# Joint 512-column matmuls for the fourth block product of the first MLP product, with its bank filled by ScalarE

## The chip, the cores and the metric

The kernel runs on one core of a Trainium2 chip. The metric is the device time of one execution in microseconds (us). One execution was also taken by the profiler; its span runs from its first instruction to its last.

## The reference, cut to what matters

One decoder layer over 512 positions with 1024 features, in float32: a combined input projection feeding a gated recurrence (HGRN2) and a block-sparse attention (MoBA), an output projection, cross-attention into 256 memory tokens, and an MLP. The change lies in the first matrix product of the MLP:

```python
h = rms_norm(x, norm_mlp[l])
x = x + jnp.square(jax.nn.relu(h @ w_ff1[l])) @ w_ff2[l]   # w_ff1: 1024 x 4096, w_ff2: 4096 x 1024
return rms_norm(x, norm_final)
```

## The kernel before

All large products work on split operands. A float32 matrix is written as an upper part, rounded to the fast matmul type (float32r), and a lower part, the rest. A product is then upper x upper, plus upper weights x lower activations, plus lower weights x upper activations. ScalarE makes the upper part of a weight tile (`wh<-w...` in the profile), VectorE subtracts it for the lower part (`wl<-w...,wh`).

The first MLP product, `h @ w_ff1`, is done with a Strassen-Winograd scheme: seven block products instead of eight. The 1024 input features, the 512 positions and the output columns are each cut in two. The work goes in eight groups, `f1_group(j)`, j = 0 to 7. A group makes all seven products p = 0 to 6 for two tiles of 128 weight columns (index b); each product sums over 512 input features, four tiles of 128 (index k). In groups 0 to 6 the products come in the order 0, 1, 2, 5, 4, 3, 6 (`F1_ORDER`); group 7 takes them in their own order. The "third" and "fourth" product are p = 2 and p = 3. Some weight blocks are sums, made by VectorE (`f1_add`) or by accumulating DMA transfers issued by GpSimd.

An activation operand `op1(p, k)` holds its upper part in 256 columns and its lower part in the 256 columns behind it. The accumulators are four tiles of two PSUM banks each, `Z`, `Y`, `XA` and `XB` (X is XA in even groups, XB in odd ones), seen as [128, 2, 512] with `lo` the first and `hi` the last 256 columns of each bank. The upper weight part is used in one of two ways (`upper`):

- joint: one matmul of 512 columns for each tile. Upper x upper lands in `lo`, upper x lower in `hi`, and both halves are added when the bank is read;
- not joint (p = 1 and 3, both in Y): two matmuls of 256 columns with the same weights, both into `lo`.

The lower weight part (`lower`) is a 256-column matmul into `lo` in either case. So a joint product has 16 matmuls and another 24. `lower_first` and `lower_last` decide whether `lower` or `upper` goes first.

Products share banks because the scheme adds them. X holds product 0, then 0+2, then 0+2+4, then 0+2+4+6. After product 0, ScalarE copies X to Z, where product 5 is added. Y holds product 1 and then 1+3. What a group leaves goes to two result tiles, `t1` and `t2` (in the profile `g`): after each product `evac(p)` has ScalarE copy one half of a bank and VectorE add other halves. `f1_tile` multiplies a finished tile by the norm's factor `rb3` with max or min (the relu, with either sign), and a square on ScalarE follows.

The order on each engine is the order in which the code issues it. Every product is a step: `need(w)` issues the split of the weights for the step after the next one, and loads of coming raw tiles; then come these lists, in this order: `post` (squares on ScalarE, by `f1_post`), a VectorE sum of weights at the third step, `first` (VectorE additions that free a bank soon), the held lower parts of the split, and `rest` (other VectorE work, by `f1_rest`). Then the step's matmuls are issued and `evac(p)`. The raw weight tiles `wA`, `wB`, `wc`, `wC`, `wD` have three buffers in each of two pools. A load into one waits until the split's lower part (or the sum) that reads its former content is done; loads go through SyncE's queue in order, accumulating transfers through GpSimd's (lines 373 and 375). GpSimd (line 240) and SyncE (line 237) also issue sums of w_ff2's blocks in DRAM, for the next stage. Most other instructions of the trace have line 118, that of a recording helper, so the groups are told apart by tile names.

Of the kernel before, what the change touches and what calls it, by code (L numbers as in the profile page):

```python
# [11 lines left out]
AF = mybir.ActivationFunctionType  # L12
ALU = mybir.AluOpType
AX = mybir.AxisListType

P = 128
# [109 lines left out]
def hybrid_layer(ctx: ExitStack, tc: tile.TileContext, xT, memT, ws, vecs, consts, rots, out):  # L126
    nc = tc.nc
    pace = Pace()
    V, A, PE = (pace.engine(e, t) for e, t in ((nc.vector, "dve"), (nc.scalar, "act"), (nc.tensor, "pe")))
# [7 lines left out]
    first = ExitStack()  # L137
# [101 lines left out]
    def add(dst, src):  # L239
        return nc.gpsimd.dma_start(dst, src, accum_op=ALU.add, max_dma_last_dim=4 * D)  # L240
# [73 lines left out]
    def load_unit():  # L314
        u = state["load"]
        raws[u] = raw_tile(f"wr{u}", u >= FF2 and (u - FF2) % 2 == 1)
        if len(sources[u].shape) == 3:
            SY.dma_start(raws[u].rearrange("p (n c) -> p n c", n=4), sources[u])
        else:
            SY.dma_start(raws[u], sources[u])  # L320
        state["load"] += 1
        for _ in range(sums_after(u)):
            more_sums()
# [34 lines left out]
    def split_unit(eng=None):  # L358
        u = split_begin()
        split_part(u, 0, D, eng)  # L360
        del raws[u]
# [7 lines left out]
    def f1_load(j, what):  # L369

        r, c = {"A": (0, 0), "B": (0, 0), "C": (1, 1), "D": (1, 0)}[what.upper()]
        t = f1raw[what, j] = raw_tile(f"w{what}{j}", what in "AD")
        nc.sync.dma_start(two(t), E[r][c][j].rearrange("n p c -> p n c"))
        if what in "Bc":
            nc.gpsimd.dma_start(two(t), E[0][1][j].rearrange("n p c -> p n c"), accum_op=ALU.add)
# [4 lines left out]
    def f1_prep(j, s):  # L380

        split_raw(split_begin(), f1raw[("ABACcDd" if j == 7 else "ABADcCD")[s], j], 0, D)
        if s == 1 and j == 0:
            f1_add(j, "A", "B", "C")
        if j == 7:
            if s == 1:
                f1_load(j, "d")
                state["load"] = FF2
            elif s > 3:
                load_unit()  # L390
        elif s == 1:
            f1_load(j + 1, "B")
        elif s == 2:
            f1_load(j + 1, "A")
        elif s == 4:
            f1_load(j + 1, "c")
        elif s == 5:
            f1_load(j + 1, "C")
        elif s == 6:
            f1_load(j + 1, "D")  # L400
        if s == 2 or s == 6 and j > 1:
            more_sums()

    def need(u):
        marks.append(last_mm[0])
        if MLP <= u + SPLIT_AHEAD < FF2:
            f1_prep(*divmod(u + SPLIT_AHEAD - MLP, 7))
            return
        last = MLP if u < MLP else UNITS
        most = RAWS if u < MLP else 2 * RAWS  # L410
        want_load, want_split = min(last, u + LOAD_AHEAD + 1), min(last, u + SPLIT_AHEAD + 1)
        while state["split"] < want_split or state["load"] < want_load:
            if state["load"] < want_load and state["load"] - state["split"] < most:
                load_unit()
            elif state["split"] < want_split:
                split_unit()
            else:
                break
        if MLP - 6 <= u < MLP - 2:
            for what in ("A", "B", "cC", "D")[u - MLP + 6]:  # L420
                f1_load(0, what)
        if MLP - 7 <= u < MLP - 2:
            more_sums()
# [124 lines left out]
    eps = cpool.tile([P, 1], F32, name="eps")  # L548
# [48 lines left out]
    for i in range(2):  # L597
        t = fp.tile([P, NT, P], F32, name=f"AT{i}")
# [694 lines left out]
    half = T // 2  # L1293
# [59 lines left out]
    def part(k, h):  # L1353

        return g[k][:, :, h * half:(h + 1) * half]

    rest = []

    def f1_tile(t, op):
        V.scalar_tensor_tensor(t, t, 0.0, rb3[:, None, :].to_broadcast([P, 2, T]), op0=op, op1=ALU.mult)  # L1360
        post.append(lambda: A.activation(t, t, AF.Square))

    def f1_end(t, j):
        k = j // 2
        f1_tile(t, ALU.max)
        if j % 2:
            subs.append(lambda: V.tensor_sub(part(k, 1), part(k + 4, 1), part(k, 1)))

    post, first, subs = [], [], []

    def f1_post():
        while post:
            post.pop(0)()

    def f1_rest():
        while rest:
            rest.pop(0)()

    lower_last = [False]

    def f1_group(j):

        X = XX[j % 2]
        t1, t2 = (g[4 * i + j // 2][:, 2 * j % 4:2 * j % 4 + 2, :] for i in range(2))
        lo, hi = slice(0, half), slice(half, T)

        def evac(p):
            def add(when, to, acc, *parts):
                for x in parts:
                    when.append(lambda x=x: V.tensor_add(to, to, acc[:, :, x]))  # L1390

            if p == 0:
                A.activation(Z, X, AF.Copy)
            elif p == 1:
                A.activation(t2[:, :, hi], Y[:, :, lo], AF.Copy)
            elif p == 2:
                A.activation(t2[:, :, lo], X[:, :, lo], AF.Copy)
                add(first, t2[:, :, lo], X, hi)
            elif p == 5:
                A.activation(t1[:, :, lo], Z[:, :, lo], AF.Copy)  # L1400
                add(rest, t1[:, :, lo], Z, hi)
            elif p == 4:
                add(first, t2[:, :, hi], X, lo, hi)
            elif p == 3:
                add(rest, t2[:, :, lo], Y, lo)
            else:
                A.activation(t1[:, :, hi], X[:, :, lo], AF.Copy)
                add(rest, t1[:, :, hi], X, hi)
                rest.append(lambda: f1_end(t1, j))
            if p == (4 if j == 7 else 3):  # L1410
                rest.append(lambda: f1_tile(t2, ALU.min))

        every = range(4)
        steps = [(p, every) for p in F1_ORDER[j]]
        if j == 0:
            steps[1:3] = [(1, range(3)), (2, range(3)), (1, range(3, 4)), (2, range(3, 4))]
        for p, ks in steps:
            at_p = F1_ORDER[j].index(p)
            if at_p == 3 and j == 0:
                nc.scalar.preload_act_table_set("natural_log_exp_and_others")  # L1420
            w = MLP + 7 * j + at_p
            if j == 0 and at_p == 4:
                drain("n3")
            if 0 in ks:
                held.append([])
                need(w)
                f1_post()
                if at_p == 2:
                    D = "Dd"[j == 7]
                    f1_add(j, D, D, "A")  # L1430
                while first:
                    first.pop(0)()
                for made_low in held.pop():
                    made_low()
                f1_rest()
                if at_p == 3 and subs:
                    subs.pop()()
                if j == 7 and at_p in (3, 5):
                    need_op(at_p // 5)
                if at_p == 5 and j < 7:  # L1440
                    f1_add(j + 1, "A", "B", "C")
                if j == 0 and at_p == 2:
                    step(made["n3"])
                    set_wait(made["n3"], 1e6)
            acc = {1: Y, 3: Y, 5: Z}.get(p, X)
            joint = p not in (1, 3)
            opens = 0 in ks and p < 2
            tiles = [(b, op1(p, k), slice(b * T + k * P, b * T + k * P + P)) for b in range(2) for k in ks]

            def upper():  # L1450
                for b, a, c in tiles:
                    first_of = opens and c.start % T == 0
                    if joint:
                        mm(acc[:, b], his[w][:, c], a, first_of, False)
                    else:
                        for x in lo, hi:
                            mm(acc[:, b, lo], his[w][:, c], a[:, x], first_of and x is lo, False)

            def lower():
                for b, a, c in tiles:  # L1460
                    mm(acc[:, b, lo], los[w][:, c], a[:, lo], False, False)

            lower_first = lower_last[0] and not opens
            for half_of in (lower, upper) if lower_first else (upper, lower):
                half_of()
            lower_last[0] = not lower_first
            if 3 in ks:
                evac(p)

# [175 lines left out]
    for p, (name, begins, after) in enumerate(PLAN):  # L1647
# [3 lines left out]
        for j in range(8):  # L1651
# [10 lines left out]
            hi, lo = his[FF2 + i], los[FF2 + i]  # L1662
# [3 lines left out]
            for part_of in parts:  # L1666
# [13 lines left out]
                opens = begins and c == 0 and part_of is parts[0]  # L1680
# [91 lines left out]
```

## Time and profile before

| | |
|---|---|
| median of 3 runs | 720.58 us |
| the three runs | 720.26, 720.58, 725.79 us |
| profiled execution, its own time | 719.96 us |
| its span | 718.1 us |
| TensorE busy in the span | 709.5 us (99%) |
| VectorE busy | 581.1 us (81%) |
| ScalarE busy | 451.4 us (63%) |
| GpSimd busy | 81.5 us (11%) |
| the first MLP product, all eight groups | 395.15 to 553.38 us, 158.23 us |

In the profile PE is TensorE's matmuls, PEld its weight loads, DVE VectorE, ACT ScalarE, POOL GpSimd, SPq SyncE's queue. A row of a group of instructions gives the operation, the tile written `<-` the tiles read (buffer numbers left out), the shape, the count, and times in us or, where they are those of one instruction, in ns. A row of the timeline gives start and length in us, and in brackets the engine's idle time before it and what ended that. TensorE's matmuls are pipelined, and a row's length covers their overlap.

### The profile page before, as it was taken

The page shows a single profiled execution, that of the slowest core. Times are in us where ns is not written, and L with a number is a line of the kernel's source. Part 1 is how long each engine was busy: PE and PEld are TensorE (multiplying, and loading weights), DVE is VectorE, ACT ScalarE, POOL GpSimd, SP SyncE. Part 2 cuts the span into 40 slices and gives each one's busy share as a digit, 9 for nine tenths or more (in the row PEclk, how much of TensorE's full clock was granted, in tenths as well). Part 3 has the DMA queues.
Part 4 walks back from the last instruction along what each step waited for, and adds up shares of the span by engine and source line. Part 5 has one row for each costly group of instructions (what it writes and reads, how often), then busy time and mean ns, then how long its engine had stood idle before and what let it go on. Part 6 is the DMA issues. An engine that isn't in the chain of part 4 may idle for free.

```text
span 718.1 us, 10752 instructions
## 1 busy us (share of the span) xinstructions
PE 709.5 (99%) x4038; PEld 613.2 (85%) x4038; DVE 581.1 (81%) x882; ACT 451.4 (63%) x654; POOL 81.5 (11%) x98
## 2 busy tenths in 40 slices
PE   9999999999999999999999999999999999999995
PEld 7888888888888888888888999999999888888885
DVE  6899537898787777767578889989899799987886
ACT  7883585446586577656565866565657665547672
POOL 2511132000000000000011111211111100110000
PEclk9999999999999999999999999999999999999998
DMA  9999699976457846453757588898899976998623
GB/s 298 273 298 303 160 177 251 364 263 141 157 174 203 259 158 193 153 177 117 235 135 162 148 204 188 221 288 244 261 237 272 301 268 199 278 279 248 191 74 117
DMA packets 63843, 155.58 MB, mean 217 GB/s; under 512 B 5264, under 2 KB 21008, under 8 KB 63280
## 3 DMA queue, kind: packets, MB, share of 16 engines
q1 hardware_dynamic: 47920, 116.43, 46.8%
q0 software_dynamic: 14592, 37.75, 28.8%
q10 hardware_dynamic: 1280, 0.72, 0.3%
q8 instruction: 31, 0.51, 0.3%
q14 instruction: 20, 0.16, 0.1%
HBM read 152.79 MB, written 48.23 MB: 280 GB/s over the span
## 4 chain that ended last, share of the span: by engine, by line
PE 98%; DMA 1%; DVE 0%; ACT 0%; DVEq 0%; SPq 0%; issue 0%; ACTq 0%
PE Y L118 16%; PE X L118 12%; PE xo L118 8%; PE XB L118 6%; PE XA L118 6%; PE mkq L118 6%; PE xq L118 6%; PE wo L118 6%; PE mv L118 3%; PE hg L118 3%; PE hq L118 3%; PE Z L118 3%; PE hf L118 3%; PE memX L118 3%; PE hi L118 3%; PE memY L118 2%
## 5 line engine op out<-in xcount | busy, mean ns | idle before, releaser
L118 DVE TENSOR_TENSOR wl<-wr,wh 128x1024 fp32r<-128x1024 f32 (+2 forms) x139 | 165.6, 1197 | 31.0 <-ACT wh L118 28.2
L118 ACT ACTIVATE wh<-wr 128x1024 fp32r<-128x1024 f32 (+2 forms) x139 | 142.8, 1036 | 74.9 <-PE Y L118 14.5
L240 POOL DMA_DIRECT2D u<-in_ws_dram x32 | 28.6, 903 | 358.3 <-PE memX L118 108.6
L118 PE MATMUL X<-op,wh 128*128 128x512 f32 (+1 forms) x264 | 62.9, 385 | 0.0
L118 PEld LDWEIGHTS X<-op,wh 128*128 128x128 f32 x264 | 47.2, 189 | 8.5
L118 PE MATMUL Y<-op,wh 128*128 128x512 f32 x192 | 47.2, 391 | 0.0
L118 PEld LDWEIGHTS Y<-op,wh 128*128 128x128 f32 x192 | 35.0, 188 | 6.6
L118 PEld LDWEIGHTS X<-op,wl 128*128 128x128 f32 x256 | 33.5, 191 | 1.6
L118 PE MATMUL X<-op,wl 128*128 128x256 f32 x256 | 34.1, 282 | 0.0
L118 PE MATMUL Y<-OS,wh 128*128 128x256 f32 x256 | 33.4, 283 | 0.0
L118 PEld LDWEIGHTS Y<-OS,wh 128*128 128x128 f32 x256 | 32.5, 192 | 0.7
L118 DVE TENSOR_TENSOR op<-g,op 128x1024 fp32r<-128x1024 f32 x24 | 29.3, 1219 | 2.8 <-ACT op L118 2.8
L118 ACT ACTIVATE op<-g 128x1024 fp32r<-128x1024 f32 x28 | 29.3, 1045 | 0.6 <-PE XB L118 0.6
L118 ACT ACT_TABLE_LOAD x20 | 25.7, 1283 | 2.2 <-issue 1.8
L118 PEld LDWEIGHTS Y<-op,wl 128*128 128x128 f32 x192 | 25.3, 191 | 1.3
L118 PE MATMUL Y<-op,wl 128*128 128x256 f32 x192 | 25.7, 282 | 0.0
L118 PE MATMUL xq<-x1hi,wl 128*128 128x512 f32 x64 | 25.6, 400 | 0.0
L118 PE MATMUL mkq<-xhi,wh 128*128 128x512 f32 x64 | 25.4, 397 | 0.0
L118 PE MATMUL mkq<-xhi,wl 128*128 128x512 f32 x64 | 25.4, 397 | 0.0
L118 PE MATMUL xq<-x1hi,wh 128*128 128x512 f32 x64 | 25.3, 396 | 0.0
L118 DVE TENSOR_TENSOR wl<-wD,wh 128x1024 fp32r<-128x1024 f32 x15 | 18.4, 1225 | 8.5 <-ACT wh L118 7.9
L118 PE MATMUL mkq<-xlo,wh 128*128 128x512 f32 x64 | 25.2, 394 | 0.0
(370 smaller groups left out, 1914.3 us busy)
## 6 DMA issues: line engine op xcount, KB each, us to landing
wr<-in_ws_dram SPq DMA_DIRECT2D x87, 512.0 KB, 4.9
u<-in_ws_dram POOLq DMA_DIRECT2D x32, 512.0 KB, 8.1
wr<-u SPq DMA_DIRECT2D x32, 512.0 KB, 4.6
u<-in_ws_dram SPq DMA_DIRECT2D x16, 512.0 KB, 10.9
wr<-m SPq DMA_DIRECT2D x16, 512.0 KB, 4.1
m<-in_ws_dram POOLq DMA_DIRECT2D x12, 512.0 KB, 10.1
m<-in_ws_dram POOLq DMA_DIRECT2D x16, 256.0 KB, 6.5
wA<-in_ws_dram SPq DMA_DIRECT2D x8, 512.0 KB, 6.4
```

What stands on the lines that cost most here:

```text
L118: return f(*args, **kw)
L240: return nc.gpsimd.dma_start(dst, src, accum_op=ALU.add, max_dma_last_dim=4 * D)
```

## The change

It has five parts. Joint matmuls for product 3 in groups 0 to 6, and for product 1 in group 0. In groups 1 to 6 ScalarE fills `lo` of Y with zeros at the group's first step, product 1 accumulates onto them instead of opening the bank, and after product 2 ScalarE copies `hi` of X into `hi` of Y, where product 3 is then added: with that, `hi` of X need not be added by VectorE any more, and that addition goes. This copy and the one of `lo` of X to t2 are put on `post`, so they stand behind the next step's split. In group 0, where Y is opened by a joint product 1, its `hi` is added to t2 by VectorE. After product 3 both halves of Y are added, on `first` instead of `rest`. And the square of t1 goes to a list of its own, run after the following group's second `evac`.

```diff
-    def f1_tile(t, op):
+    def f1_tile(t, op, when):
...
-        post.append(lambda: A.activation(t, t, AF.Square))
+        when.append(lambda: A.activation(t, t, AF.Square))
...
-        f1_tile(t, ALU.max)
+        f1_tile(t, ALU.max, ready if j < 7 else post)
...
             elif p == 1:
                 A.activation(t2[:, :, hi], Y[:, :, lo], AF.Copy)
+                if j == 0:
+                    add(rest, t2[:, :, hi], Y, hi)
             elif p == 2:
-                A.activation(t2[:, :, lo], X[:, :, lo], AF.Copy)
-                add(first, t2[:, :, lo], X, hi)
+                if 0 < j < 7:
+                    post.append(lambda: A.activation(Y[:, :, hi], X[:, :, hi], AF.Copy))
+                    post.append(lambda: A.activation(t2[:, :, lo], X[:, :, lo], AF.Copy))
+                else:
+                    A.activation(t2[:, :, lo], X[:, :, lo], AF.Copy)
+                    add(first, t2[:, :, lo], X, hi)
...
             elif p == 3:
-                add(rest, t2[:, :, lo], Y, lo)
+                add(first if j < 7 else rest, t2[:, :, lo], Y, *((lo, hi) if j < 7 else (lo,)))
...
-                rest.append(lambda: f1_tile(t2, ALU.min))
+                rest.append(lambda: f1_tile(t2, ALU.min, post))
...
                 need(w)
+                if p == 0 and 0 < j < 7:
+                    A.activation(Y[:, :, lo], eps[:, :, None].to_broadcast([P, 2, half]), AF.Copy, scale=0.0)
                 f1_post()
...
-            joint = p not in (1, 3)
-            opens = 0 in ks and p < 2
+            joint = j == 0 or p != 1 and (j < 7 or p != 3)
+            opens = 0 in ks and (p == 0 or j in (0, 7) and p == 1)
...
-            lower_first = lower_last[0] and not opens
+            lower_first = lower_last[0] and p > 1
...
             if 3 in ks:
                 evac(p)
+                while behind:
+                    behind.pop(0)()
+                behind.extend(ready)
+                ready.clear()
```

More of the change, by code (lines that the diff above doesn't have):

```diff
@@ L1357, in hybrid_layer @@
     rest = []
-    def f1_tile(t, op):
+    def f1_tile(t, op, when):
         V.scalar_tensor_tensor(t, t, 0.0, rb3[:, None, :].to_broadcast([P, 2, T]), op0=op, op1=ALU.mult)
-        post.append(lambda: A.activation(t, t, AF.Square))
+        when.append(lambda: A.activation(t, t, AF.Square))
     def f1_end(t, j):
         k = j // 2
-        f1_tile(t, ALU.max)
+        f1_tile(t, ALU.max, ready if j < 7 else post)
         if j % 2:
             subs.append(lambda: V.tensor_sub(part(k, 1), part(k + 4, 1), part(k, 1)))
-    post, first, subs = [], [], []
+    post, ready, behind, first, subs = [], [], [], [], []
     def f1_post():
```

## The prediction

> **What bounds the kernel now.** I began with the page: what is busy, and which engine carries the chain that ended last.
>
> ```profile
> span 718.1 us, 10752 instructions
> PE 709.5 (99%) x4038; PEld 613.2 (85%) x4038; DVE 581.1 (81%) x882; ACT 451.4 (63%) x654; POOL 81.5 (11%) x98
> PE 98%; DMA 1%; DVE 0%; ACT 0%; DVEq 0%; SPq 0%; issue 0%; ACTq 0%
> ```
>
> TensorE is busy for 99% of the span and holds 98% of the chain. The other engines matter only where they make it wait. Then I cut the changed stage, the first MLP product, into its eight groups (j = 0 to 7) by windows. Columns: window, its length, busy time of each engine with instruction counts, granted clock, DMA share, GB/s. The rows are j = 2, 3 and 4 and the sum of all eight.
>
> ```profile
> 435.26:454.95 19.69, 19.69 (x129) 18.06 (x129) 18.05 (x19) 12.10 (x14) 4.24 (x4) 1.00 0.83 211
> 454.95:474.63 19.68, 19.68 (x129) 18.05 (x129) 16.34 (x17) 12.10 (x14) 3.37 (x3) 1.00 0.95 251
> 474.63:494.32 19.69, 19.69 (x130) 18.06 (x129) 18.68 (x20) 12.10 (x14) 2.39 (x2) 1.00 0.95 257
> sum 158.23, PE 158.21 PEld 144.86 DVE 141.87 ACT 101.97 POOL 24.70; mean PE 19.78 PEld 18.11 DVE 17.73 ACT 12.75 POOL 3.09
> ```
>
> The stage takes 158.23 us and TensorE is busy for 158.21 of it, at clock 1.00. So there is no wait here to be won. Only TensorE's own work can shrink, and only a new wait can cost. VectorE is nearly full (up to 18.68 of 19.69), ScalarE is not (12.1), and the DMA share reaches 0.95.
>
> **TensorE, step by step.** The chain lists each product of a group as one row: start, length, bank, matmuls. These are j = 3 from product 0 on, and above them the end of j = 2.
>
> ```profile
> 449.27 2.87 PE Y L118 x24
> 452.15 2.80 PE XA L118 x16
> 454.95 2.77 PE XB L118 x16
> 457.71 2.88 PE Y L118 x24
> 460.59 2.80 PE XB L118 x16
> 463.39 2.77 PE Z L118 x16
> 466.16 2.80 PE XB L118 x16
> 468.96 2.87 PE Y L118 x24
> ```
>
> Products 1 and 3 (bank Y) are the 24-matmul steps: 16 of 256 columns for the weights' upper part, 8 of 256 for the lower part. The others run 8 of 512 and 8 of 256. A 256-column matmul thus takes 2.875/24 = 0.1198 us. A step of 2.77 leaves (2.77 - 8 x 0.1198)/8 = 0.2265 us for a 512-column one. Two of the first cost 0.2396 us, one of the second 0.2265: 0.0131 us saved per pair. Steps that begin with the lower part take 2.80 instead of 2.77. Product 3 begins with the upper part, after a product that ended with the upper part, exactly as product 5 (Z) does, so 2.77 is its row. The order of parts stays as it was in every group: I walked the new condition (p > 1) through j = 0, 1 and 7, and it gives the old sequence.
>
> **What the change removes on TensorE.** Product 3 becomes joint in j = 0 to 6, product 1 in j = 0: 8 products, 64 pairs. By steps: 8 x (2.87 - 2.77) = 0.80 us. By pairs: 64 x 0.0131 = 0.84 us. A second reading, busy time of the groups by shape:
>
> ```profile
> L118 PE MATMUL Y<-OS,wh 128*128 128x256 f32 x256 | 33.4, 283 | 0.0
> L118 PE MATMUL Z<-OB,wh 128*128 128x512 f32 x64 | 15.8, 389 | 0.0
> ```
>
> 2 x 33.4/256 - 15.8/64 = 0.0141 us, or 0.90 us for 64 pairs. I take **0.8 us**, with 0.7 and 0.9 as ends. That all 158 us are TensorE-bound makes this gain arrive in full if nothing new waits.
>
> The Trainium skill (TensorE: Matmul & The Clock Gate, Back-to-back issue gap) gives an isolated warm matmul of N columns N/2.4 + 2.5 ns. By this rule a pair would save only the fixed 2.5 ns, and the whole change about 0.16 us, an estimate from that page. The trace does not agree: by it both kinds of step would take about 2.6 us, 0.02 apart, where the chain has 2.87 and 2.77.
>
> **What it adds on ScalarE.** In j = 1 to 6: a fill of Y's first half (2 x 256 columns) with zeros, and a copy of X's second half into Y. The trace has no fill, so I bound it: below by the smallest write into Y, above by a write of twice the size; nearest is the 512-element copy.
>
> ```profile
> L118 ACT ACTIVATE Y<-x,vec x3: 462/462/463, 703.1 to 708.7; 128x256 f32<-128x256 f32 x3
> L118 ACT ACTIVATE g<-XA x8: 598/598/604, 403.6 to 533.7; 128x512 f32<-128x512 f32 x8
> L118 ACT ACTIVATE Z<-XA x4: 1006/1008/1008, 398.0 to 516.9; 128x1024 f32<-128x1024 f32 x4
> ```
>
> I take 0.60 us for each, ends 0.46 and 1.01. That is 1.2 us a group on an engine with 7.6 us idle, so only the places count. Here is ScalarE through j = 3, with TensorE's first matmuls of products 1, 2 and 4.
>
> ```profile
> 454.99 0.60 ACT L118 ACTIVATE g<-XA 128x512 f32<-128x512 f32 x1 [4.61 <-PE XA L118]
> 455.48 1.05 ACT L118 ACTIVATE wh<-wA 128x1024 fp32r<-128x1024 f32 x1
> 456.71 1.06 ACT L118 ACTIVATE g<-g 128x1024 f32<-128x1024 f32 x1 [0.18 <-DVE g L118]
> 457.55 2.08 PE L118 MATMUL Y<-OS,wh 128*128 128x256 f32 x16
> 457.81 1.01 ACT L118 ACTIVATE Z<-XB 128x1024 f32<-128x1024 f32 x1
> 460.43 1.12 PE L118 MATMUL XB<-OS,wl 128*128 128x256 f32 x8
> 460.67 0.58 ACT L118 ACTIVATE g<-Y 128x512 f32<-128x512 f32 x1
> 466.00 1.12 PE L118 MATMUL XB<-OS,wl 128*128 128x256 f32 x8
> ```
>
> - **The fill** stands behind the split of wA (ends 456.53) and ahead of the square of t2. It runs 456.53 to 457.13. Product 1 starts at 457.55: **0.42 us to spare**, and with the long end, 1.01, still 0.01. This is a new wait of TensorE, and it is the thinnest place. Queued behind the fill on ScalarE are the square of t2 and the copy Z<-XB.
> - **VectorE** gives the fill its go: the two additions out of Y now come first in the last step of a group, ahead of the split's lower part instead of one addition behind it.
>
> ```profile
> 409.33 1.22 DVE L118 TENSOR_TENSOR wl<-wD,wh 128x1024 fp32r<-128x1024 f32 x1 [1.45 <-ACT wh L118]
> 453.60 1.22 DVE L118 TENSOR_TENSOR wl<-wB,wh 128x1024 fp32r<-128x1024 f32 x1
> 454.74 0.68 DVE L118 TENSOR_TENSOR g<-g,Y 128x512 f32<-128x512 f32 x1
> 455.45 1.22 DVE L118 SCALAR_TENSOR_TENSOR g<-g,rb 128x1024 f32<-128x1024 f32 x1
> 464.06 0.69 DVE L118 TENSOR_TENSOR g<-g,XB 128x512 f32<-128x512 f32 x1 [0.60 <-ACT g L118]
> 467.83 1.23 DVE L118 TENSOR_TENSOR wl<-wD,wh 128x1024 fp32r<-128x1024 f32 x1 [1.60 <-ACT wh L118]
> 472.71 1.23 DVE L118 TENSOR_TENSOR wA<-wB,wC 128x1024 f32<-128x1024 f32 x1 [0.59 <-DMA wC<-in_ws_dram]
> ```
>
> The additions, 2 x 0.68, would run 453.60 to about 454.96, so the fill, at 456.53, does not wait for them. The multiplication of t2 by rb, now at 455.45, ends about 0.6 to 0.7 us later, near 457.3. The addition at 464.06 goes (ScalarE's copy replaces it), so a group has as many VectorE instructions as before, and the idle 0.60 and 1.60 us in these rows swallow the shift each group. Group 0 alone gets two additions more, 1.4 us, in front of a wait of its own (1.45 us for ScalarE, the row at 409.33); I cost them at nothing, 1.4 us if that cover were gone.
> - **ScalarE onward, late by this**: square of t2 457.32 to 458.38, Z<-XB to 459.39 (product 2 writes XB at 460.43: 1.0 to spare), split of wD to 460.44, the copy of product 1 at 460.67 as now, then the square of t1 (moved behind that copy) to 462.31, splits of wc and wC to 463.36 and 464.41, and now the two copies out of X, to 465.01 and 465.61. Product 4 writes X at 466.00: **0.39 us to spare**. Product 3, in the chain at 468.96, needs the copy in Y three microseconds later still. VectorE's lower part of wc follows the split at 463.36 and ends near 464.6, 1.4 us ahead of product 4, which begins with it.
> - **Queues.** The raw tile wB comes free with VectorE's lower part, 1.3 us later. SyncE's load into it, the load of wA behind it in that queue, GpSimd's accumulating transfer and the DRAM sum queued behind that move too.
>
> ```profile
> 454.85 0.37 SPq L373 DMA_DIRECT2D wB<-in_ws_dram  x1
> 461.79 1.23 POOL L375 DMA_DIRECT2D wB<-in_ws_dram  x1 [8.71 <-DMA wB<-in_ws_dram]
> 469.00 1.06 ACT L118 ACTIVATE wh<-wB 128x1024 fp32r<-128x1024 f32 x1 [0.25 <-PE XB L118]
> 475.17 1.05 ACT L118 ACTIVATE wh<-wA 128x1024 fp32r<-128x1024 f32 x1
> DMA to landing us min/median/max: 3.8/5.6/7.0
> ```
>
> The accumulating transfer of 461.79 lands at 468.8 at the latest (7.0). Moved by 1.3 it lands at 470.1, so ScalarE's split at 469.00 may be 1.1 us late, inside the 4.6 us that ScalarE idles before the group's end. VectorE uses wB for the sum at 472.71, where it waits for wC already. So nothing reaches TensorE.
>
> **The sum.** 719.96 us is the profiled execution, 718.1 of it span and 1.86 around it. Span: 718.1 - 0.8 + 0 = 717.3, hence 719.16 for an execution like that one. The median shown, 720.58, lies 0.62 above the profiled execution, so on its scale the forecast is 720.58 - 0.8 = **719.8 us**.
>
> **Rivals.**
> 1. **A late weight reaches TensorE through the fill (slower).** Before, product 1 asked nothing of ScalarE's queue at that point. Now the fill stands behind the split of wA, which needs the sum wA<-wB,wC, which needs two transfers that now start up to 1.3 us later while the DMA share is 0.95. For: the 0.59 us wait for wC at 472.71. Against: that sum ends at 473.94 and the split begins at 475.17, 1.23 us to spare, plus 0.42 behind the fill. It decides from a sum 1.65 us late on; each us beyond is a us of TensorE. Late by 2.2 us in j = 2 to 6, it costs 5 x 0.55 = 2.75 us: 722.5 us.
> 2. **The copies out of X hold product 4.** Only 0.39 us to spare; with copies of 0.9 us instead of 0.60, twice, product 4 waits 0.2 us, six times: 1.2 us, so 721.0 us. Against: the 598 ns row moves the same shape.
> 3. **A matmul costs its columns alone**, and the 24-matmul steps are longer for another reason, such as the bank they write: then a pair saves nothing and the time stays at 720.6 us. Against: 0.10 us lie between the steps of Y and Z throughout. With the page's 2.5 ns for each pair it would be 720.4 us.
>
> That the change doesn't do what it says is not open: the condition for joint matmuls stands in the diff.
>
> **How the numbers follow.** Forecast 0.75; rival 1 0.10; rival 2 0.09; rival 3 0.06. The range takes the forecast's ends (0.7 and 0.9) and the spread of undisturbed executions, 719.96 to 720.58 here, on both sides, and reaches over rivals 2 and 3: 718.9 to 721.3. Rival 1 and part of the spread are left out. About 1% (7 us) is what a measurement of this kernel can tell from no change; none of the cases comes to that: faster 0.01, same 0.97, slower 0.02. Inside "same" I put 0.75 on a gain too small to be told from the scatter of a few runs.
>
> **What would show it.** Right: 64 matmuls Y<-OS,wh of 512 columns and 128 of 256, product 3 in the chain as x16 with 2.77 us, groups 1 to 6 of 19.58 to 19.60 us, group 0 some 0.2 shorter, two more ScalarE writes into Y a group at about 0.60 us, TensorE with no idle time in the stage. Wrong: TensorE waiting for ScalarE at Y (product 1: rival 1) or at X (product 4: rival 2), or a step of product 3 that stays at 2.85 (rival 3). What I could not see is whether ScalarE's writes into a bank beside TensorE's stream slow either; Z<-XB does that today without a trace in the 2.77 us steps.

## The result and the profile after: some 7 us slower

| | before | after |
|---|---|---|
| median (lowest to highest, executions) | 720.46 us (719.97 to 725.79, 8) | 727.61 us (725.49 to 730.0, 8) |
| profiled execution, its span | 719.96, 718.1 us | 728.66, 726.8 us |
| start of group 0 to end of group 6 (its length) | 394.99 to 533.53 us (138.54) | 395.80 to 541.15 us (145.35) |

The ratio is 1.0086 (95% interval 1.0065 to 1.0106). A group runs here from the first matmul of its product 0 to that of the next group's. Of the 8.7 us between the two spans, 6.81 lie in groups 0 to 6, 0.81 ahead of them, where the code is the same, and 1.08 behind them.

The page of the kernel after: span, busy time of each engine, and the engines' shares of the chain that ended last.

```profile
span 726.8 us, 10627 instructions
PE 714.0 (98%) x3974; PEld 613.7 (84%) x3974; DVE 580.7 (80%) x884; ACT 456.8 (63%) x666; POOL 81.4 (11%) x98
PE 82%; DMA 8%; DVE 6%; ACT 2%; issue 2%; DVEq 0%; POOL 0%; ACTq 0%; POOLq 0%
```

TensorE has 64 matmuls fewer (3974 for 4038), as the change says. But it holds 82% of the chain instead of 98%; DMA and VectorE have entered it. The windows of the kernel after show where: groups 1 to 5 and the sum of groups 0 to 6 (same columns as before).

```profile
416.67:436.25 19.58, 19.58 (x121) 17.64 (x120) 16.42 (x18) 12.86 (x16) 3.33 (x3) 1.00 0.75 191
436.25:455.83 19.58, 19.58 (x121) 17.64 (x120) 16.46 (x18) 12.86 (x16) 3.46 (x4) 1.00 0.87 203
455.83:476.63 20.80, 20.09 (x121) 17.75 (x120) 16.60 (x17) 12.93 (x16) 4.13 (x4) 1.00 0.87 196
476.63:501.99 25.36, 22.43 (x121) 20.30 (x120) 20.17 (x21) 13.36 (x17) 2.39 (x2) 0.87 0.96 254
501.99:521.57 19.58, 19.58 (x121) 17.64 (x120) 16.30 (x17) 12.99 (x16) 2.39 (x2) 1.00 0.83 229
sum 145.35, PE 141.49 PEld 126.02 DVE 122.91 ACT 92.39 POOL 20.52; mean PE 20.21 PEld 18.00 DVE 17.56 ACT 13.20 POOL 2.93
```

Groups 1, 2 and 5 take 19.58 us, the forecast's number (19.69 before). Against 19.58, group 3 loses 1.22 and group 4 loses 5.78. Group 0 took 20.87 us for 20.42 before: its product 0, whose code is unchanged, waited for VectorE's `OA`. What TensorE meets in group 4, by the timelines of TensorE and ScalarE after (the first ScalarE row is an undisturbed fill, in group 1):

```profile
482.49 3.78 PE L118 MATMUL Y<-OS,wh 128*128 128x256 f32 x16 [2.93 <-ACT Y L118]
418.32 0.59 ACT L118 ACTIVATE Y<-eps 128x512 f32<-128x512 f32 x1
480.57 1.06 ACT L118 ACTIVATE wh<-wA 128x1024 fp32r<-128x1024 f32 x1 [3.14 <-DVE wA L118]
481.84 0.60 ACT L118 ACTIVATE Y<-eps 128x512 f32<-128x512 f32 x1 [0.20 <-DVE g L118]
```

Product 1 waits 2.93 us for the fill, the fill stands behind the split of wA, and the split waited 3.14 us for VectorE's sum. The rest of the 5.78, 2.85 us, is clock. The granted clock is 0.87 over the whole group, but two windows over product 1 of group 4 show 0.50 right behind the wait:

```profile
482.49:486.07 3.58, 3.58 (x17) 3.58 (x17) 3.55 (x5) 1.96 (x3) 0.00 (x0) 0.50 0.62 145
486.07:488.00 1.93, 1.93 (x11) 1.93 (x11) 1.91 (x2) 0.98 (x2) 0.12 (x1) 0.50 1.08 334
```

The upper part of product 1 takes 3.78 us there for the 2.08 of before. Group 3's loss begins with two short waits, 0.20 us for the fill and 0.51 for the copy Z<-XB that product 2 needs. All waits of TensorE after for ScalarE in this stage (total, times, longest):

```profile
PE Y L118 <- ACT Y L118: 3.1, 2, 2.9
PE XB L118 <- ACT Z L118: 0.5, 1, 0.5
```

The chain of waits after tells why the sum was late. The short steps between a sum and the next load are left out; the last row is product 3 of the same group, now 16 matmuls in 2.77 us, as forecast.

```profile
427.51 7.13 DMA wC<-in_ws_dram
...
434.77 1.23 DVE wA L118
...
447.39 8.22 DMA wC<-in_ws_dram
...
455.73 1.23 DVE wA L118
...
468.35 10.79 DMA wC<-in_ws_dram
...
479.26 1.22 DVE wA L118
...
481.84 0.61 ACT Y L118
482.49 5.49 PE Y L118 x24
...
496.59 2.77 PE Y L118 x16
```

This is a **loop that goes round TensorE**. A load of wC lands (434.64), the sum runs, then on VectorE and ScalarE the additions, t2's multiplication, a copy, a split and the lower parts, which free the buffer of the next wC, and its load starts at 447.39: 12.75 us from landing to next issue. The next turn has 12.74 (455.61 to 468.35). A group takes 19.58 us, so a turn keeps pace while wC lands within 19.58 - 12.75 = **6.83 us**. It took 7.13, 8.22 and 10.79. The sum's wait for wC grew in step (VectorE's timeline after):

```profile
434.77 1.23 DVE L118 TENSOR_TENSOR wA<-wB,wC 128x1024 f32<-128x1024 f32 x1 [0.83 <-DMA wC<-in_ws_dram]
455.73 1.23 DVE L118 TENSOR_TENSOR wA<-wB,wC 128x1024 f32<-128x1024 f32 x1 [2.20 <-DMA wC<-in_ws_dram]
479.26 1.22 DVE L118 TENSOR_TENSOR wA<-wB,wC 128x1024 f32<-128x1024 f32 x1 [4.93 <-DMA wC<-in_ws_dram]
```

SyncE's load into wB, which by the prediction would go 1.3 us later, went later with every group: 2.23, 3.60 and 6.34 us from the start of groups 2, 3 and 4. SyncE's queue after, then before (loads of wc and wC):

```profile
438.48 0.37 SPq L373 DMA_DIRECT2D wB<-in_ws_dram  x1
446.25 0.37 SPq L373 DMA_DIRECT2D wc<-in_ws_dram  x1
447.39 0.37 SPq L373 DMA_DIRECT2D wC<-in_ws_dram  x1
459.43 0.37 SPq L373 DMA_DIRECT2D wB<-in_ws_dram  x1
482.97 0.38 SPq L373 DMA_DIRECT2D wB<-in_ws_dram  x1
```

```profile
443.80 0.37 SPq L373 DMA_DIRECT2D wc<-in_ws_dram  x1
446.58 0.37 SPq L373 DMA_DIRECT2D wC<-in_ws_dram  x1
```

The loads of wc and wC, 512 KB each, now start 1.14 us apart; here it was 2.78 before. The median landing of wC in the stage (last number, us), before and after:

```profile
wC<-in_ws_dram SPq DMA_DIRECT2D x7, 512.0 KB, 4.3
```

```profile
wC<-in_ws_dram SPq DMA_DIRECT2D x7, 512.0 KB, 6.9
```

So the landing went from 2.5 us below the loop's limit to just above it. TensorE feels nothing for two groups, until the lateness has eaten the slack ahead of the fill; its stall then lets the loads catch up, and group 5 is clean.

### The profile page after: what moved, and what is told of

It is laid out like the page before. It is cut to its first block, busy times and chain, and to the rows that moved or that the text cites. A ratio compares the mean times of both kernels' runs of the same rounds, so it can differ in the third digit from the quotient of the medians.

```text
span 726.8 us, 10627 instructions
## 1 busy us (share of the span) xinstructions
PE 714.0 (98%) x3974; PEld 613.7 (84%) x3974; DVE 580.7 (80%) x884; ACT 456.8 (63%) x666; POOL 81.4 (11%) x98
## 4 chain that ended last, share of the span: by engine, by line
PE 82%; DMA 8%; DVE 6%; ACT 2%; issue 2%; DVEq 0%; POOL 0%; ACTq 0%; POOLq 0%
PE Y L118 13%; PE X L118 10%; PE mkq L118 6%; PE xq L118 6%; PE wo L118 6%; PE xo L118 5%; DMA wC<-in_ws_dram 4%; PE XA L118 3%; PE hf L118 3%; PE mv L118 3%; PE hg L118 3%; PE hq L118 3%; PE memX L118 3%; PE hi L118 3%; PE XB L118 3%; DMA wr<-in_ws_dram 2%
## 5 line engine op out<-in xcount | busy, mean ns | idle before, releaser
L118 PE MATMUL Y<-OS,wh 128*128 128x256 f32 (+1 forms) x192 | 34.5, 331 | 3.1 <-ACT Y L118 3.1
L118 PEld LDWEIGHTS Y<-OS,wh 128*128 128x128 f32 x192 | 29.4, 202 | 6.2 <-ACT Y L118 3.5
```

What stands on the lines that cost most here:

```text
L118: return f(*args, **kw)
```

## The experiments

Theories: **R** (later also **L**), the later release of buffers, turned into the loop above; its rival **S**, the new order on ScalarE; and from the third series on **D** (**D2**), transfers that are slower because TensorE's program is shorter. Times are in us; each ratio is to the kernel before in the same series, whose medians were 720.08 to 720.53. "Wait" is the longest wait of the sum wA<-wB,wC for wC. "x" is the median landing of the eight first loads of x, at the very start, ahead of everything that differs. The medians are of 2 executions for e9, of 4 for e8 and e11, and of 5 to 12 for the others except e10. Base A is the kernel after, B the kernel before.

| run | base, edit | median | ratio (95%) | groups 3, 4 | wait | x |
|---|---|---|---|---|---|---|
| before | | 720.46 | | 19.68, 19.69 | 0.6 | 6.4 |
| after | | 727.61 | 1.0086 (1.0065-1.0106) | 20.80, 25.36 | 4.9 | 7.1 |
| e1 | A, additions behind | 725.84 | 1.0070 (1.0043-1.0096) | 20.54, 21.36 | 2.4 | 7.2 |
| e2 | B, late lower part | 723.59 | 1.0027 (1.0006-1.0049) | 19.69, 23.52 | 5.4 | 6.3 |
| e3 | A, fill first | 727.24 | 1.0077 (1.0047-1.0107) | 20.18, 23.77 | 5.2 | 7.1 |
| e4 | A, old ScalarE order | 728.33 | 1.0095 (1.0065-1.0125) | 19.84, 24.03 | 4.9 | 7.2 |
| e5 | A, sums early | 723.99 | 1.0043 (1.0028-1.0057) | 19.58, 19.58 | 0.4 | 6.8 |
| e6 | B, sums early | 720.97 | 1.0010 (1.0001-1.0019) | 19.69, 19.69 | none | 6.2 |
| e7 | A, e1 + e4 | 724.72 | 1.0060 (1.0046-1.0074) | 19.85, 21.47 | 2.5 | 7.1 |
| e8 | A, matmuls in halves | 723.19 | 1.0042 (1.0025-1.0058) | 19.96, 22.06 | 3.5 | 6.5 |
| e9 | B, 64 matmuls fewer at the end | 725.46 | 1.0072 (1.0052-1.0092) | 19.69, 24.38 | 5.2 | 7.1 |
| e10 | B again, one execution | 719.78 | | 19.68, 19.69 | 1.5 | 6.1 |
| e11 | A, 128 GpSimd writes | 725.80 | 1.0069 (1.0049-1.0089) | 20.65, 22.31 | 3.7 | 7.1 |
| e12 | A, 64 small matmuls at the end | 723.38 | 1.0036 (1.0023-1.0048) | 19.80, 21.46 | 2.9 | 6.2 |
| e13 | A, e5 + e12 | 723.05 | 1.0047 (1.0023-1.0070) | 19.58, 19.58 | none | 6.5 |
| e14 | A, e7 + e12 | 723.07 | 1.0032 (1.0020-1.0045) | 19.58, 20.57 | 1.6 | 6.4 |
| e15 | B, e12's edit | 721.57 | 1.0018 (1.0000-1.0036) | 19.69, 19.69 | 0.7 | 6.6 |
| e16 | A, e7 + e18 | 721.96 | 1.0013 (0.9992-1.0033) | 19.58, 19.58 | 2.5 | 6.1 |
| e17 | B, sums spread | 723.05 | 1.0025 (1.0007-1.0043) | 19.68, 19.69 | 4.0 | 6.2 |
| e18 | A, sums spread + e12 moved | 721.70 | 1.0014 (0.9996-1.0032) | 19.58, 19.58 | 2.4 | 6.2 |

**First series: which part of the change starts it.** e1 puts the fourth product's additions back behind the split's lower part; e3 issues the fill ahead of the split of wA; e4 takes back the new places of the copies and the square on ScalarE; e2 leaves the kernel before as it was and makes only one lower part late.

```diff
 # e1 (on after)
-                add(first if j < 7 else rest, t2[:, :, lo], Y, *((lo, hi) if j < 7 else (lo,)))
+                add(rest, t2[:, :, lo], Y, *((lo, hi) if j < 7 else (lo,)))
 # e2 (on before)
-                for made_low in held.pop():
+                lows = held.pop()
+                if at_p == 6 and j < 7:
+                    f1_rest()
+                for made_low in lows:
                     made_low()
 # e3 (on after)
-                need(w)
                 if p == 0 and 0 < j < 7:
                     A.activation(Y[:, :, lo], eps[...], AF.Copy, scale=0.0)
+                need(w)
 # e4 (on after; f1_end's square goes to post again, too)
-                    post.append(lambda: A.activation(Y[:, :, hi], X[:, :, hi], AF.Copy))
-                    post.append(lambda: A.activation(t2[:, :, lo], X[:, :, lo], AF.Copy))
+                    A.activation(Y[:, :, hi], X[:, :, hi], AF.Copy)
+                    A.activation(t2[:, :, lo], X[:, :, lo], AF.Copy)
```

> The changed kernel with one line undone: the two VectorE additions of product 3 go back to the later list (rest), behind the lower part of wB. Theory R (release): the additions ahead of that lower part hold the raw tile wB 1.3 us longer, its load and the accumulating transfer behind it start late, the five loads of a group bunch, wC lands late, and the split of wA and the fill behind it make TensorE wait. Then this kernel has no wait of VectorE for wC over 0.6 us, groups 1 to 6 of 19.58 us and 719.7 us. Theory S (ScalarE order): what hurts is that ScalarE is about 1 us later in the middle of a group, so that wc is split, freed and loaded late; then wC still lands late here and the time stays at 724 us or more.

> The kernel before with one move: in the last step of a group the lower part of wB is issued behind the addition out of Y and the multiplication by rb, so wB is free 1.9 us later; no joint product, no fill, no copy. Theory R: VectorE's wait for wC grows to 2 us and more in the middle groups, as in the changed kernel; TensorE, which has no fill to wait for, loses only what outlasts the 3 us to product 2's lower weights: 720.5 to 723 us. Theory S: nothing changes, 720.5 us and waits for wC as in the kernel before (0.6 us).

> The changed kernel with the fill issued ahead of the split of wA instead of behind it. Theory R with the fill as the last link: the late sums stay (VectorE waits 2 to 5 us for wC), but product 1 no longer waits for ScalarE at Y; product 2 waits only for what exceeds its 3 us, so 720 to 723 us. If the late sums reach TensorE by another way, the time stays at 725 to 728 us. Theory S: waits for wC unchanged, time as by R.

> The changed kernel with ScalarE's old order: the square of t1 ahead of the copy of product 1, and the two copies out of X straight after product 2, ahead of the next split. Fill, joint products and VectorE's order as in the changed kernel. Theory R: no help, VectorE's waits for wC of 2 us and more stay, 724 to 728 us. Theory S: the waits go, 719.7 us.

e2 has no fill and no new joint product, yet it falls into the same loop. Its window of group 4, and its chain of waits from one load of wC to the next and on to TensorE's product 1:

```profile
475.15:498.67 23.52, 21.40 (x130) 19.59 (x128) 19.55 (x20) 12.08 (x14) 2.39 (x2) 0.93 0.88 260
```

```profile
447.25 7.34 DMA wC<-in_ws_dram
...
467.48 10.63 DMA wC<-in_ws_dram
...
478.23 1.23 DVE wA L118
...
480.20 4.53 PE Y L118 x24
```

From landing (454.59) to the next issue are 12.89 us here, so wC has 6.80 of the 19.69 us of a group, and took 7.34 and 10.63. Its wB loads start 2.46 and 2.67 us from the start of groups 1 and 2, for 0.62 and 0.07 before. A later release alone is enough, then: R holds for e2, and the old schedule has nearly the same limit. S falls with e4: with ScalarE's old order the waits for wC reach the same 4.9 us. e3 tells that the fill's place behind the split isn't the cause either: there the fill waits for VectorE's additions (7.6 us in four waits), which stand behind the late sum as well, and the 720 to 723 us expected became 727.24. e1 missed what R gave for it (no wait above 0.6 us, 719.7 us): its wB load started on time in group 1 (0.61 us after the group's start), and still the sum waited 1.95, 1.58 and 2.38 us in groups 2 to 4. So the early additions are not the whole cause.

**Second series: the load on the DMA.** e5 and e6 move twelve of the w_ff2 sums, 512 KB DRAM transfers issued within groups 0 to 6, ahead of the stage, in the new and the old schedule. e7 is e1 and e4 together.

```diff
 # e5, e6
-        if s == 2 or s == 6 and j > 1:
+        if j == 7 and s in (2, 6):
             more_sums()
...
+        if MLP - 16 <= u < MLP - 4:
+            more_sums()
```

> The changed kernel with 12 of the w_ff2 block sums in DRAM (those issued in groups 0 to 6) issued one per weight unit in the two stages before instead, so that groups 0 to 6 share the DMA with nothing. All else as changed. Theory L (a loop through a nearly full DMA: late release, late load, late wC, late sum, late VectorE, later release): with the contention gone the lateness of 1.3 us is absorbed, VectorE's waits for wC vanish in every group, groups 1 to 6 take 19.58 us and the time is 719 to 720 us, if the stages before carry the sums without loss. Rival C (the VectorE and ScalarE orders alone make TensorE wait, whatever the DMA does): waits of TensorE at Y stay and the time stays above 724 us.

> The kernel before with the same 12 sums moved early: the control for the run beside it. Theory L: the kernel before hardly waits there, so 720 to 720.5 us, and its occasional runs of 722 to 725 us become rarer; the difference to the run beside it is the matmul's gain, 0.8 us. If the move itself costs something in the stages before, it shows here.

> The changed kernel with both orders undone: product 3's additions behind the lower part of wB, the square of t1 and the copies out of X at their old places on ScalarE. Left are the joint products, the fill, the copy and one addition moved within the group. Theory L: the loads keep nearly their old times (wB 0.1 us and wc about 9.3 us after a group's start), so the loop starts seldom: 719.7 to 722 us. Rival F (the fill's wait for VectorE, now behind the lower part, reaches TensorE in any group where the sum is a little late): 723 us or more, with TensorE waiting at Y.

The windows of groups 3 and 4 of e5:

```profile
456.98:476.56 19.58, 19.58 (x121) 17.64 (x120) 16.68 (x18) 12.98 (x16) 2.36 (x2) 1.00 0.75 185
476.56:496.14 19.58, 19.58 (x121) 17.64 (x120) 17.71 (x19) 12.98 (x16) 2.36 (x2) 1.00 0.75 186
```

With a DMA share of 0.75 instead of 0.87 and 0.96 the loop is gone, and groups 0 to 6 take 137.82 us against e6's 138.55: the change's matmul gain arrives, 0.73 us. TensorE's matmuls wait for no engine in these groups, so rival C falls. But the whole kernel, expected at 719 to 720 us, is still 3 us behind e6. In e5's profile the stage begins 1.8 us later than in e6's, behind code that both share. So there is a second cause, outside the stage. e7 missed 719.7 to 722 us, too. Its 724.72 us and its TensorE waits at Y (2.1 us in two) are what rival F named, but they stand behind sums that waited 2.51 and 1.24 us for wC.

**Third series: slower transfers.** The loads of x start at once, in identical code. Their row in the kernel before, and in the kernel after:

```profile
xraw<-in_xT_dram SPq DMA_DIRECT2D x8, 256.0 KB, 6.4
```

```profile
xraw<-in_xT_dram SPq DMA_DIRECT2D x8, 256.0 KB, 7.1
```

What differs there is the length of TensorE's program: 64 matmuls and their 64 weight loads fewer. e8 gives the count back within the stage (the newly joint matmuls issued as two of 256 columns, which forgoes the 0.8 us), e9 takes 64 matmuls from the end of the kernel before (lower parts of the last block product, which are left out), e11 gives the whole program 128 instructions of GpSimd instead, and e10 is the kernel before once more.

```diff
 # e8 (on after)
-                    if joint:
+                    if joint and (p == 3 or p == 1):
+                        for x in lo, hi:
+                            mm(acc[:, b, x], his[w][:, c], a[:, x], first_of and x is lo, False)
+                    elif joint:
                         mm(acc[:, b], his[w][:, c], a, first_of, False)
 # e9 (on before)
-                    for k, a, w in part_of:
+                    for k, a, w in part_of if i < 48 else ():
 # e11 (on after; pad is a small tile of its own)
+            if i == 32:
+                for _ in range(128):
+                    nc.gpsimd.memset(pad, 0.0)
```

> The changed kernel with each 512-column matmul of the newly joint products issued as two of 256 columns, one into each half of the bank: TensorE has the instructions and the 24-matmul steps of the kernel before, all else (fill, copies, orders) is as changed. Theory L (the loop through late releases): the waits for wC and at Y are as in the changed kernel, and the time is 0.8 us longer, 727 to 729 us. Theory D (transfers are slower in the changed program as such, seen already in its first 30 us, whose code is the same: its loads of x took 7.1 us where those of the kernel before took 6.4; something in how the program lies in memory): with as many instructions as before, x lands in 6.2 to 6.4 us, product hi starts at 28.2 to 28.8 us, the loop starts later or not at all, and the time is 720.5 to 724 us.

> The kernel before without the 64 matmuls of the lower weight part in the last block product of the second MLP product (left out, so the output lacks that part): 64 matmuls and 64 weight loads fewer, as many as the change takes away, but at the very end. TensorE has 7.7 us less to do there, so 712.8 us. Theory D: the first loads of x land in 7 us, product hi starts at 29.0 us or later, and waits for wC appear in the first MLP product, 714 us or more. Theory L: the start and the first MLP product are those of the kernel before, 712.8 us.

> The kernel before, unchanged: a second profile of it. Theory D: x lands in 6.2 to 6.4 us again and product hi starts near 28.2 to 28.8 us; a start of 29 us or more here would mean that the difference at the start is scatter between executions and not the program's.

> The changed kernel with 128 tiny memsets on GpSimd, issued in the second MLP product where GpSimd idles: the total of instructions is that of the kernel before again, no work on any path. Theory L: as the changed kernel, 726 to 729 us. Theory D, if the total is what counts: x lands in 6.4 us or less and the time falls to 720.5 to 724 us; if TensorE's own instructions count, it stays.

e9 is the telling one, though its end didn't get the 7.7 us shorter that I expected (VectorE and ScalarE bound it there: the part behind group 6 took 184.3 us for 184.6 before). Its stage has the old schedule unchanged. The row of x in e9, its window of group 4, and its sum there:

```profile
xraw<-in_xT_dram SPq DMA_DIRECT2D x8, 256.0 KB, 7.1
```

```profile
475.26:499.64 24.38, 21.39 (x129) 19.59 (x128) 19.94 (x20) 12.20 (x14) 2.39 (x2) 0.93 0.92 249
```

```profile
478.07 1.22 DVE L118 TENSOR_TENSOR wA<-wB,wC 128x1024 f32<-128x1024 f32 x1 [5.17 <-DMA wC<-in_ws_dram]
```

A shorter TensorE program slowed transfers more than 650 us ahead of the place where it was shortened, and the old schedule, otherwise unchanged, lost 4.69 us in group 4. Not every transfer is slower: the 54 loads of wr by SyncE between 30 and 390 us have a median landing of 4.6 us in the kernel before and 4.7 in e9. But in groups 0 to 2, with the same schedule, wC's is 4.7 and 5.1 us in before and e10, and 6.0 in e9. e8's x lands in 6.5 us, e11's in 7.1: TensorE's count matters, GpSimd's doesn't replace it.

**Fourth series: the count given back at the end.** e12 adds 32 tiny float32 products (64 matmuls and 64 weight loads) behind the last sum of the norm; e13, e14 and e15 do the same on e5, e7 and the kernel before.

```diff
 # e12 (on after), e15 (on before)
-        sums = [bank2(tag)[:, 0, :P] for tag in ("Y0", "X0")]
+        both = [bank2(tag) for tag in ("Y0", "X0")]
+        sums = [t[:, 0, :P] for t in both]
...
             smm(ps, ones, q[:, c], False, True)
+        for _ in range(32):
+            smm(both[1][:32, 1, :32], ones[:, :32], ones[:, :32], True, True)
```

> The changed kernel with 32 tiny float32 matmuls (64 matmul and 64 weight-load instructions) on TensorE at the very end, after its last sum, while other engines finish: TensorE has as many instructions as in the kernel before. Theory D2 (TensorE's own instruction count, or how its program then lies in memory, sets how fast transfers go from the first microsecond on): x lands in 6.1 to 6.5 us, product hi starts at 28.0 to 28.8 us, and the time is that of the two-halves kernel less the matmul's 0.8 us: 722 to 723 us. Against D2 (the two-halves kernel was better for another reason, such as the even pace of TensorE): 726 to 728 us, x in 7.1 us.

> The run with the block sums moved early, with the same tiny matmuls at the end. D2 and the loop together: groups 1 to 6 of 19.58 us, x in 6.1 to 6.5 us, and 720.2 us, that is the kernel before with early sums (720.97) less 0.8. Against D2: 724 us as without the tail.

> The run with both orders undone, with the same tiny matmuls at the end. D2 and the loop: loads nearly at their old times and transfers at their old speed, so few waits: 719.7 to 721.5 us. Against D2: 724.7 us as without the tail.

> The kernel before with the same tiny matmuls at the end: 128 TensorE instructions more than before instead of fewer. If more instructions are as good or better: x in 6.1 to 6.5 us and 720 to 720.5 us. If any change of the count moves the program to a worse place: x in 7 us and 721 to 724 us. It also shows that the tiny matmuls themselves cost nothing at the end.

e12's loads of x, groups 3 and 4, and what the small matmuls cost at the end:

```profile
xraw<-in_xT_dram SPq DMA_DIRECT2D x8, 256.0 KB, 6.2
```

```profile
454.47:474.27 19.80, 19.80 (x122) 17.70 (x120) 15.60 (x17) 12.87 (x16) 3.36 (x3) 1.00 0.91 216
474.27:495.73 21.46, 20.09 (x122) 17.75 (x120) 20.09 (x21) 13.09 (x16) 2.39 (x2) 1.00 0.94 269
```

```profile
714.40 0.37 ACT L118 ACTIVATE rb<-X,eps 128x128 f32<-128x128 f32 x1 [1.66 <-PE X L118]
```

Instructions added at the very end made the kernel after 4.2 us faster. They were not free, though that was expected; less their own 1.66 us (1.25 by the medians of e15 and of before in its series) the kernel would stand at 721.7 to 722.1, 1.4 to 1.8 above that before. So by this pair **5.3 to 5.8 of the 7.15 us go with the slower transfers**, which also feed the loop. e8 against e11, a pair of the third series, gives less: 2.6 us, and 3.4 with the gain that e8 forgoes. The share is thus known only as 3 to 6 us. What e12 leaves agrees with its stage: 0.22 + 1.88 us of loop in groups 3 and 4, less the gain of 0.7 to 0.8.

e13's stage is clean (137.82 us for groups 0 to 6) and begins at 395.72 us, as e6's does (395.66). Its profiled execution took 721.16, by estimate 719.5 without the tail's 1.66. But its median missed the 720.2 us expected, its executions reached from 720.95 to 728.97, and why isn't settled. e14 missed as well: group 4 still loses 0.99 us, behind a sum that waited 1.6, so something is left of the loop or of F.

**Fifth series: sums spread.** One sum each of groups 2, 3 and 4 goes to groups 0 and 1; in e16 and e18 the 64 matmuls stand where nothing waits for them.

```diff
 # e16, e17, e18
-        if s == 2 or s == 6 and j > 1:
+        if s == 2 or s == 6 and j in (0, 1, 5, 6, 7) or s == 4 and j == 0:
             more_sums()
```

> The changed kernel with both causes met: the two orders undone, TensorE's instruction count restored by 32 tiny matmuls at the end (now into a bank that nobody reads afterwards, so they cost nothing there), and one of the two w_ff2 block sums of groups 2, 3 and 4 moved to groups 0 and 1, where the DMA has room. If the two causes are all there is: x lands in 6.1 to 6.5 us, groups 1 to 6 of 19.58 us, no wait of TensorE at Y, 719.5 to 720.0 us, 0.4 to 0.8 less than the kernel before. If something else still costs: 721 us or more.

> The kernel before with the same three sums moved: the control. 720.0 to 720.5 us; the sums cost nothing in groups 0 and 1. The difference to the first run of this call is the gain of the matmuls, 0.8 us in the trace.

> The changed kernel, its orders as they are, with the same tiny matmuls at the end and the same three sums moved. If the late releases alone (wB 1.4 us later) are harmless once the DMA has room in groups 2 to 4 and transfers go at the old speed: 719.5 to 720.5 us. If the loop still starts: waits for wC over 1 us in group 3 or 4 and 721 to 723 us.

All three missed the 719.5 to 720.5 us of their main theories. Group 2 of e17, then of e18:

```profile
435.66:457.76 22.10, 20.17 (x130) 18.16 (x129) 20.18 (x21) 12.09 (x14) 2.40 (x2) 1.00 0.97 258
```

```profile
434.78:455.82 21.04, 20.08 (x122) 17.72 (x121) 20.09 (x21) 13.09 (x16) 2.40 (x2) 1.00 1.00 262
```

The loop moved with the sums, to group 2, with a DMA share of 0.97 and 1.00, in the old schedule too (e16's group 2 took 21.44 us). With x landing alike (6.2 us) and the sums at the same places, the new schedule is no slower than the old one (721.70 and 723.05), but no version beat the kernel before.

## Why the prediction was wrong

- **The gain on TensorE was right.** Product 3 is one x16 step of 2.77 us in the chain, undisturbed groups take 19.58 us, and e5 and e13 show 0.73 us for groups 0 to 6 against e6. Group 0 gave less than forecast: 0.08 us (20.34 in e1, e5 and e12, for 20.42), not 0.2. The fill took 0.59 us for 0.60, wB's load starts about 1.4 us later in undisturbed groups (1.43 us from the start of e5's groups 2 and 3, for 0.07), and no copy out of X held product 4 (rival 2): TensorE's waits for ScalarE are at product 1 and once at product 2. Product 3 now takes 0.1 us less in the same bank, which rules out rival 3.
- **The step that failed is "So nothing reaches TensorE", in the part on queues**, which costed late loads at nothing. I followed the shift of 1.3 us once through SyncE's and GpSimd's queues, found 1.1 us of it inside ScalarE's idle time, and stopped. I didn't ask whether the last thing it delays (the release of wC's buffer) is also the first thing that it depends on. It is: in a group of 19.58 us, a turn of 12.75 us leaves only 6.83 for the landing. The landing went from 4.3 to 6.9 us (median), and the term that stands as 0 in the forecast's sum became 1.22 + 5.78 us in groups 3 and 4; with the transfers at their old speed (e12) it was still 2.1 us. The bunching of wc and wC, 1.14 us apart, was in no step either. It slows wC without slow transfers: where x lands in 6.1 to 6.6 us, wC's median landing is 3.7 to 4.8 us where the two loads start 1.7 to 2.8 us apart (before, e6, e10, e14 to e17), except for e2 with its late loads (6.1), and 5.3 to 5.9 where they start 1.14 apart (e8, e12, e13, e18). e9, with the old spacing and slow transfers, has 6.0.
- **Rival 1 named the path** (late wC, sum, split of wA, fill, product 1), and its point of decision was about right: a sum 1.65 us late. In group 4 the sum waited 4.93 us, 4.34 more than before; that is 2.7 beyond 1.65, and TensorE waited 2.93. Wrong was its size: a constant 2.2 us in five groups (722.5 us) instead of lateness that builds up over groups and breaks in one. The prediction had the wait of 0.59 us at 472.71 as its sign, set 1.23 + 0.42 us of slack against it, and gave it 0.10. Read with e10 (1.5 us at the same place, at no cost) and with e2, e9 and e17, that wait was a sign that the old schedule stands close to the same loop.
- **The clock after a wait was not priced.** 2.93 us of wait cost another 2.85 in group 4, at a granted clock of 0.50 during product 1.
- **A term of 3 to 6 us stood in no step.** The slower transfers come from the program, not from the schedule; no row of the trace of before could show them. e8, e9 and e12 show that they go with the length of TensorE's program: 128 instructions fewer brought them, the same number given back took them away. More than the old number gained nothing (e15, x in 6.6 us). Why is open: the count itself, the placement of code in memory and its fetching weren't told apart.

## What to carry to other kernels

When an edit delays a buffer's release, follow it until it comes back to itself: add up the turn from landing to next issue, subtract it from the period, and compare what is left with the landing times under load, not with an idle engine's slack. Here the sign was a wait of 0.59 us on a transfer (1.54 in e10) at a DMA share of 0.95. And before explaining a slowdown by the schedule, compare a transfer at the start, in code that both programs share; if it differs, restore the instruction count in a control.

## What the runs showed of the hardware

- The eight loads of x land in 6.1 to 6.6 us in all 12 profiles of programs with the full count of TensorE instructions or more, and in 6.8 to 7.2 us in all 8 of programs with 128 fewer, without overlap. On one and the same chip e2 and e6 had 6.3 and 6.2, and e1, e3, e4, e5 and e7 had 6.8 to 7.2, so it isn't a matter of the chip. 128 more on GpSimd changed nothing (e11, 7.1).
- Waits of TensorE of 2.1 to 3.0 us lowered the granted clock in their window to 0.93 (e2, e9) and 0.87 (after, with 0.50 during the product behind the wait); two waits of 0.86 and 0.51 us in group 4 of e12 left it at 1.00. The Trainium skill (TensorE: Matmul & The Clock Gate, What's actually happening) has the clock halve after an idle window of about 3.4 us that runs freely. The halving is seen here, too, but shorter waits were enough: behind the 2.99 us of e9's group 4, product 1 took 4.60 us instead of 2.88.
